# Hybrid decoder trunk: the last four experts gather their rows of X and store them over `out`; all tiles of X are loaded and stored plainly, with the loads during those experts

## The chip, the cores and the metric

The kernel runs on one core of one Trainium2 chip. The metric is the device time of one execution in microseconds (us), given as the median of several runs; two kernels are compared on the same chip.

## The reference, cut to what matters

One layer of a decoder trunk (2048 tokens, width 1024): a gated linear attention mixer, then a mixture of 64 experts in 8 groups, where each token takes two experts of one group; both are added to the residual x. A final RMSNorm gives the output.

```python
def rmsnorm(x, g):
    x32 = x.astype(jnp.float32)
    y = x32 * lax.rsqrt(jnp.mean(x32 * x32, axis=-1, keepdims=True) + EPS)
    return (y * g.astype(jnp.float32)).astype(x.dtype)
...
def hier_moe(h, w_group, w_expert, w1, w3, w2):
...
    g_sel = jnp.argmax(g_logits, axis=-1)
...
    e_prob = jax.nn.softmax(e_logits[tok, g_sel], axis=-1)
    top_p, top_i = lax.top_k(e_prob, MOE_TOPK)
...
    def expert_block(args):
        xb, e = args
        hid = jax.nn.silu(xb @ w1[e]) * (xb @ w3[e])
        return hid @ w2[e]
...
    out = jnp.zeros((n_tok + 1, dm), ys.dtype).at[slot_tok].add(ys)[:n_tok]
...
def reference(x, ...):
...
        x = x + m.astype(x.dtype)
        h = rmsnorm(x, ffn_norm[i])
        x = x + hier_moe(h, moe_w_group[i], moe_w_expert[i], moe_w1[i], moe_w3[i], moe_w2[i]).astype(x.dtype)
    return rmsnorm(x, final_norm)
```

## The kernel before

The program has four stages. The mixer (`phase_gla`) and the output projection with the router (`phase_out`) come first; the latter leaves the residual in the DRAM tensor `s["X"]` (2048 x 1024, float32), the normed rows in `s["h"]`, and in SBUF `tok` and `gate`: for each expert a column of up to 96 token numbers (a number that is no token marks an empty place) and their gates.

`phase_moe` is the third stage. Its loop runs over the experts e = 0 to 63 and one step more. Work is written out in the order in which each engine is to take it, and each engine takes its instructions strictly in that order. In step e, TensorE (PE) does the first half of expert e's up projection, turns expert e-1's hidden values (`htrans`), turns the gathered rows of expert e+1 (`xtrans`), does the second half of up, and then the down projection of expert e-1 (`down_mm`). ScalarE (ACT) and VectorE (DVE) split the weights, which arrive as tiles of 1 MB in float32, into a high and a low part (`ex.split`, L1157 and L1160), so that three matmuls replace one in float32. GpSimd (POOL) gathers the rows of expert e+4 from `s["h"]` (L1192) as soon as `xtrans(e + 1)` has freed the buffer, and adds the result of expert e-2 onto its rows of `s["X"]` (`scatter`, L1246), from the buffers `ys`. Its DMAs all go through one queue, the software queue (q0). SyncE (SP) issues the plain DMAs, in this stage the weights (L1152), through its own queue (q1). The weights live in 19 tiles of 128 x 2048 ("wide"), handed out and freed in the order of the program. When the loop is done, the last two results are scattered.

The fourth stage is `phase_more` and `phase_tail`. `phase_more` is a loop on the device over blocks of tokens that didn't fit the 96 places of an expert; with these inputs it runs no block, and its branch is skipped after all engines and all DMAs have been waited for. `phase_tail` then loads the 16 tiles of `s["X"]` (128 x 1024 each, L1396), squares and sums each on ACT (L1401), makes the inverse root for four tiles at a time (`root` on DVE and ACT, `refine` on DVE, L1406 to L1418), scales on DVE (`norm`, L1422) and stores each tile to `out` (L1423).

Of the kernel before, what the change touches and what calls it, by code (L numbers as in the profile page):

```python
# [21 lines left out]
S = 2048  # L22
# [35 lines left out]
NTAIL = 29  # L58
# [1112 lines left out]
def phase_moe(tc, c, a, s, ex, plan, rest):  # L1171
    nc = tc.nc
    with ExitStack() as ctx:
# [10 lines left out]
        scat = []  # L1184
# [55 lines left out]

        def down(e):
            Y[e] = ys[e % YS]
            nc.scalar.activation(Y[e][0:CAP, :], PD[e][0:CAP, :], AF.Copy, scale=s["gate"][0:CAP, ORDER[e]:ORDER[e] + 1])  # L1243

        def scatter(e):
            st = nc.gpsimd.indirect_dma_start(  # L1246
                out=s["X"], out_offset=bass.IndirectOffsetOnAxis(ap=tok[:, ORDER[e]:ORDER[e] + 1], axis=0),
                in_=Y[e], in_offset=None, bounds_check=S - 1, oob_is_err=False, compute_op=OP.add)
            for i, o in enumerate(scat):
# [23 lines left out]
        for e in range(E + 1):  # L1273
            live = e < E
            if e > 1:
                down(e - 2)
                scatter(e - 2)
            if live:
                up(e, 0)
# [16 lines left out]
            if e:  # L1296
                down_mm(e - 1)
            if e == 2:
                s["plan"] = plan_more(tc, s, plan)
        down(E - 1)  # L1300
        scatter(E - 1)


def plan_more(tc, s, one):
# [25 lines left out]
    total = one.tile([1, 1], I32, name="total")  # L1330
    nc.vector.tensor_copy(total, end[0:1, E - 1:E])
# [4 lines left out]
def phase_more(tc, c, a, s, slots):  # L1336

    nc = tc.nc
    with ExitStack() as ctx:
        ps = ctx.enter_context(tc.tile_pool(name="o_ps", bufs=1, space=PSUM, reuse_waits="tile"))  # L1340
        ident = c["ident"]
        tl, total, tab = s["plan"]
        w = [slots.tile(F32) for _ in range(6)]
        x, xt, y, small = own = [slots.tile(F32) for _ in range(4)]
        hid, ht = small[:, 0:FF], small[:, FF:2 * FF]
        nc.vector.memset(x, 0.0)
        n = nc.values_load(total[0:1, 0:1], min_val=0, max_val=E)
        with tc.For_i(0, n, 1) as i:
            SP = [mybir.EngineType.SP]
            e = nc.values_load(tl[0:1, bass.ds(i * 2, 1)], engines=SP, min_val=0, max_val=E - 1)  # L1350
            b = nc.values_load(tl[0:1, bass.ds(i * 2 + 1, 1)], engines=SP, min_val=0, max_val=(SLOTS - CAP) // MORE - 1)
            for k in range(6):
                nc.sync.dma_start(w[k], a["w_moe"][bass.ds(e, 1), k // 2, :, k % 2 * D:(k % 2 + 1) * D].rearrange("o p f -> p (o f)"))
            nc.sync.dma_start(tab, s["table"][CAP * E:].rearrange("(b p e) w -> b p e w", p=MORE, e=E)[
                bass.ds(b, 1), :, bass.ds(e, 1), :].rearrange("b p e w -> p (b e w)"))
            nc.gpsimd.indirect_dma_start(
                out=x, out_offset=None, in_=s["h"], in_offset=bass.IndirectOffsetOnAxis(ap=tab[:, 0:1], axis=0),
                bounds_check=S - 1, oob_is_err=False)
            for j in range(2):
                p = ps.tile([128, 512], F32, name="p", bufs=2)  # L1360
                for k in range(4):
                    nc.tensor.transpose(p[:, k * 128:(k + 1) * 128], x[:, (4 * j + k) * 128:(4 * j + k + 1) * 128], ident)
                nc.scalar.activation(xt[:, j * 512:(j + 1) * 512], p, AF.Copy)
            pu = ps.tile([128, 512], F32, name="pu")
            for k in range(NK):
                nc.tensor.matmul(pu, xt[:, k * 128:(k + 1) * 128], w[k // 2][:, k % 2 * 512:(k % 2 + 1) * 512],
                                 start=(k == 0), stop=(k == NK - 1))
            nc.scalar.activation(hid, pu[:, 0:FF], AF.Silu)
            nc.vector.tensor_tensor(hid, hid, pu[:, FF:], op=OP.mult)
            p = ps.tile([128, 256], F32, name="pt")  # L1370
            for k in range(2):
                nc.tensor.transpose(p[:, k * 128:(k + 1) * 128], hid[:, k * 128:(k + 1) * 128], ident)
            nc.scalar.activation(ht, p, AF.Copy)
            for j in range(2):
                p = ps.tile([128, 512], F32, name="p", bufs=2)
                for k in range(2):
                    nc.tensor.matmul(p, ht[:, k * 128:(k + 1) * 128], w[4 + k][:, j * 512:(j + 1) * 512],
                                     start=(k == 0), stop=(k == 1))
                nc.scalar.activation(y[:, j * 512:(j + 1) * 512], p, AF.Copy, scale=tab[:, 1:2].bitcast(F32))
            nc.gpsimd.indirect_dma_start(  # L1380
                out=s["X"], out_offset=bass.IndirectOffsetOnAxis(ap=tab[:, 0:1], axis=0),
                in_=y, in_offset=None, bounds_check=S - 1, oob_is_err=False, compute_op=OP.add)
        slots.free(*w, *own)


def phase_tail(tc, c, a, s, slots, gf):
    nc = tc.nc
    GRP = 4
    with ExitStack() as ctx:
        sm = ctx.enter_context(tc.tile_pool(name="t_sm", bufs=2, side="right", reuse_waits="tile"))  # L1390
        junk = [slots.tile(F32) for _ in range(2)]
        X, SS, R = {}, {}, {}

        def load(t):
            X[t] = slots.tile(F32)
            nc.sync.dma_start(X[t], s["X"][t * 128:(t + 1) * 128, :])  # L1396

        def square(t):
            if t % GRP == 0:
                SS[t // GRP] = sm.tile([128, GRP], F32, name="ssq")  # L1400
            nc.scalar.activation(junk[t % 2], X[t], AF.Square, accum_out=SS[t // GRP][:, t % GRP:t % GRP + 1])  # L1401

        def root(g):

            v = sm.tile([128, GRP], F32, name="v")
            nc.vector.tensor_scalar(v, SS[g], 1.0 / D, EPS, op0=OP.mult, op1=OP.add)  # L1406
            y = sm.tile([128, GRP], F32, name="r")
            nc.scalar.activation(y, v, AF.Ln)
            nc.scalar.activation(y, y, AF.Exp, scale=-0.5)
            R[g] = v, y  # L1410

        def refine(g):
            v, y = R[g]
            u = sm.tile([128, GRP], F32, name="u")
            nc.vector.tensor_tensor(u, y, y, op=OP.mult)
            nc.vector.tensor_tensor(u, u, v, op=OP.mult)
            nc.vector.tensor_scalar(u, u, -0.5, 1.5, op0=OP.mult, op1=OP.add)
            nc.vector.tensor_tensor(y, y, u, op=OP.mult)  # L1418

        def norm(t):  # L1420
            g, i = divmod(t, GRP)
            nc.vector.scalar_tensor_tensor(X[t], X[t], R[g][1][:, i:i + 1], gf, op0=OP.mult, op1=OP.mult)  # L1422
            nc.sync.dma_start(a["out"][t * 128:(t + 1) * 128, :], X[t])  # L1423

        NG = NT // GRP
        for t in range(NT):
            load(t)
        nc.scalar.preload_act_table_set(LN_EXP)
        for t in range(GRP):
            square(t)  # L1430
        root(0)
        refine(0)
        for t in range(GRP, 2 * GRP):
            square(t)
        for g in range(NG):
            if g + 1 < NG:
                root(g + 1)
                for t in range((g + 2) * GRP, min((g + 3) * GRP, NT)):
                    square(t)
            for i in range(GRP):  # L1440
                if i == GRP // 2 and g + 1 < NG:
                    refine(g + 1)
                norm(g * GRP + i)
# [3 lines left out]
def trunk(ctx, tc, a):  # L1447
# [7 lines left out]
        "todo": dram.tile([128, 2], I32, name="s_todo"),  # L1455
        "X": dram.tile([S, D], F32, name="s_X"),
# [22 lines left out]
    with ExitStack() as main:  # L1479
        big = main.enter_context(tc.tile_pool(name="tails", bufs=NTAIL, side="left", reuse_waits="tile"))  # L1480
        slots = Slots()
        slots.add(big, NTAIL)
        gf = slots.tile(F32)
        nc.sync.dma_start(gf, bass.AP(tensor=a["final_norm"].tensor, offset=a["final_norm"].offset, ap=[[0, 128], [1, D]]))
        phase_more(tc, c, a, s, slots)
        phase_tail(tc, c, a, s, slots, gf)
# [41 lines left out]
```

## Time and profile before

| | us |
|---|---|
| median of 3 runs (1597.9 to 1598.13) | 1597.99 |
| the profiled execution: its own time | 1600.11 |
| the profiled execution: its span | 1598.3 |
| PE busy in the span | 1514.1 |
| DVE / ACT / POOL busy | 1096.7 / 957.0 / 365.9 |

The span runs from the first to the last instruction of the profiled execution; the profiled execution's own time has 1.8 us more around it. Times in the views are counted from the span's start. The experts take the stretch from about 961 to 1546 us, the last stage the rest.

### The profile page before, as it was taken

What the parts mean: (1) busy time and instruction counts of PE and PEld (TensorE: products, weight loads), DVE (VectorE), ACT (ScalarE), POOL (GpSimd) and SP (SyncE); (2) the same over time, 40 slices, a digit from 0 to 9 for tenths busy, and PEclk for the clock granted to TensorE, in tenths of its full rate; (3) what the DMA queues carried; (4) which work ended last, traced back from release to release, by engine and by line L of the source; (5) the groups of instructions that cost most, each with busy time, mean ns of one, the idle gap of its engine ahead of it and who ended that gap; (6) DMA issues with size and microseconds to landing.
All of it is one profiled execution on the core that took longest, in us unless ns stands there. A gap on an engine that the chain in (4) does not pass through costs nothing.

```text
span 1598.3 us, 21450 instructions
## 1 busy us (share of the span) xinstructions
PE 1514.1 (95%) x7619; PEld 1197.2 (75%) x7619; DVE 1096.7 (69%) x2087; ACT 957.0 (60%) x1498; POOL 365.9 (23%) x265
## 2 busy tenths in 40 slices
PE   9999999999999999998999969999999999999960
PEld 7877888888888888877888856777777777777740
DVE  5566665566556655553655558889998998989955
ACT  6666644454445544441222238888888888888854
POOL 3211000000000000130111144535444444454320
PEclk9999999999999999999999979999999999999985
DMA  8645944434333433347488556999999999999969
GB/s 305 227 158 200 341 144 150 145 139 181 120 117 138 174 123 124 132 138 265 174 278 276 212 218 237 386 391 396 390 390 394 394 396 393 386 393 394 392 189 392
DMA packets 113213, 415.24 MB, mean 260 GB/s; under 512 B 23585, under 2 KB 40066, under 8 KB 88530
## 3 DMA queue, kind: packets, MB, share of 16 engines
q1 hardware_dynamic: 90242, 379.72, 61.3%
q0 software_dynamic: 19744, 33.85, 8.4%
q8 instruction: 60, 0.98, 0.2%
q10 hardware_dynamic: 3120, 0.30, 0.2%
q14 instruction: 47, 0.39, 0.1%
HBM read 353.92 MB, written 93.41 MB: 280 GB/s over the span
## 4 chain that ended last, share of the span: by engine, by line
PE 88%; DVE 5%; DMA 3%; ACT 2%; issue 1%; SPq 0%; POOL 0%; DVEq 0%; POOLq 0%; ACTq 0%
PE pm L832 9%; PE pu L77 7%; PE pu L76 7%; PE pu L75 7%; PE pvr L75 7%; PE pvr L76 7%; PE pvr L77 7%; PE pd L76 4%; PE pd L75 4%; PE pd L77 4%; PE ptr L1203 3%; PE pk L75 2%; PE pq L75 2%; PE pq L76 2%; PE pq L77 2%; PE pk L76 2%
## 5 line engine op out<-in xcount | busy, mean ns | idle before, releaser
L1160 DVE TENSOR_TENSOR wide<-wide 128x2048 fp32r<-128x2048 f32 x192 | 435.0, 2286 | 55.4 <-ACT wide L1157 46.8
L1157 ACT ACTIVATE wide<-wide 128x2048 fp32r<-128x2048 f32 x192 | 362.7, 1908 | 6.8 <-PE pd L76 6.4
L1246 POOL DMA_INDIRECT s_X<-y,tok x64 | 187.5, 2929 | 297.8 <-ACT y L1243 283.3
L75 PE MATMUL pu<-wide,xhi 128*96 128x512 f32 x512 | 207.0, 404 | 0.9 <-ACT xhi L66 0.9
L76 PE MATMUL pu<-wide,xhi 128*96 128x512 f32 x512 | 202.5, 396 | 2.2 <-DVE wide L1160 2.2
L77 PE MATMUL pu<-wide,xlo 128*96 128x512 f32 x512 | 203.6, 398 | 0.0
L75 PE MATMUL pvr<-big 128*128 128x512 f32 x504 | 201.2, 399 | 0.0
L76 PE MATMUL pvr<-big 128*128 128x512 f32 x504 | 197.1, 391 | 0.0
L77 PE MATMUL pvr<-big 128*128 128x512 f32 x504 | 196.8, 391 | 0.0
L832 PE MATMUL pm<-big 128*128 128x512 f32 x672 | 163.4, 399 | 5.4 <-DVE big L910 5.4
L67 POOL TENSOR_TENSOR big<-big 128x1024 fp32r<-128x1024 f32 x16 | 39.3, 2468 | 517.6 <-ACT big L66 458.2
L832 PEld LDWEIGHTS pm<-big 128*128 128x128 f32 x672 | 126.0, 191 | 31.4 <-DVE big L910 5.8
L77 PEld LDWEIGHTS pu<-wide,xlo 128*96 128x96 f32 x512 | 83.2, 162 | 36.7 <-DVE xlo L67 0.6
L75 PEld LDWEIGHTS pvr<-big 128*128 128x128 f32 x504 | 94.6, 188 | 20.5
L77 PEld LDWEIGHTS pvr<-big 128*128 128x128 f32 x504 | 94.6, 188 | 20.3
L76 PEld LDWEIGHTS pu<-wide,xhi 128*96 128x96 f32 x512 | 83.7, 164 | 34.5 <-DVE wide L1160 2.9
L66 ACT ACTIVATE sp<-st 128x256 fp32r<-128x256 f32 x64 | 26.7, 417 | 136.5 <-DVE st L455 124.4
L76 PEld LDWEIGHTS pvr<-big 128*128 128x128 f32 x504 | 94.7, 188 | 18.0
L75 PEld LDWEIGHTS pu<-wide,xhi 128*96 128x96 f32 x512 | 83.3, 163 | 32.6 <-ACT xhi L66 1.2
L75 PE MATMUL pd<-wide,ht 128*96 128x512 f32 x256 | 100.8, 394 | 1.3 <-ACT ht L66 1.3
L77 PE MATMUL pd<-wide,ht 128*96 128x512 f32 x256 | 100.7, 393 | 0.0
L76 PE MATMUL pd<-wide,ht 128*96 128x512 f32 x256 | 100.6, 393 | 0.0
(298 smaller groups left out, 2860.6 us busy)
## 6 DMA issues: line engine op xcount, KB each, us to landing
wide<-w_moe SPq DMA_DIRECT2D x192, 1024.0 KB
big<-s_hT SPq DMA_DIRECT2D x96, 512.0 KB
s_hT<-big SPq DMA_DIRECT2D x32, 512.0 KB
s_oT<-big SPq DMA_DIRECT2D x32, 512.0 KB
big<-s_oT SPq DMA_DIRECT2D x32, 512.0 KB
big<-x SPq DMA_DIRECT2D x20, 512.0 KB
big<-w_vr SPq DMA_DIRECT2D x16, 512.0 KB
s_X<-big SPq DMA_DIRECT2D x16, 512.0 KB
```

The costliest lines, as they stand in the source:

```text
L66: nc.scalar.activation(hi, src, AF.Copy)
L67: eng.tensor_tensor(lo, src, hi.bitcast(F32), op=OP.subtract)
L75: nc.tensor.matmul(out, x[0], w[0], start=start, stop=False)
L76: nc.tensor.matmul(out, x[0], w[1], start=False, stop=False)
L77: nc.tensor.matmul(out, x[1], w[0], start=False, stop=stop)
L832: self.nc.tensor.matmul(pm[i], xo[:, sl], w[:, i * 512:(i + 1) * 512], start=(k == 0 and w is whi and xo is hi), stop=(k == NK - 1 and xo ...
L1157: self.nc.scalar.activation(hi, r, AF.Copy)
L1160: self.nc.vector.tensor_tensor(lo, r, hi.bitcast(F32), op=OP.subtract)
L1203: nc.tensor.transpose(p[:, k, 0:CAP], x[0:CAP, k * 128:(k + 1) * 128], ident[0:CAP, 0:CAP])
L1246: st = nc.gpsimd.indirect_dma_start(out=s["X"], out_offset=bass.IndirectOffsetOnAxis(ap=tok[:, ORDER[e]:ORDER[e] + 1], axis=0), in_=Y[e], ...
```

## The change

The fourth stage is gone as a stage of its own, and its work is written into the end of `phase_moe`.

- The experts 60 to 63 (`LAST = 4`) no longer scatter onto `s["X"]`. Their rows of `s["X"]` are gathered (`xgather`, in steps 60 and 61) into the buffers `ys` and `xbs[1]`; DVE adds gate times result onto them (`final`, in place of `down` on ACT), ACT squares them (`final_square`), and after the closing norm (`final_norm`, DVE) GpSimd stores the rows to `out` by their numbers (`put_out`), after the 16 plain stores, whose stale rows they replace.
- The 16 tiles of `s["X"]` are loaded in eight loads of 1 MB into freed weight tiles (`load_final`, from step 61 on). They wait for the last scatter, that of expert 59.
- The squares of the tiles 0 and 1 stand in step 63 on ACT, those of 2 to 15 behind the loop, mixed with `root`, `refine` and `norm`.
- `targets` (step 3) and `targets_in` (step 6) are new. The first writes the numbers of all tokens to a DRAM tensor `s["dst"]` and overwrites those of the last four experts' tokens; the second brings them back into SBUF, turns them on PE and copies them to `dst`. With `MASK = False`, nothing reads `dst`.
- The loop over blocks that didn't fit now stands at the very end, inside a branch that is taken only if there are such blocks, and then does the closing norm over.

```diff
+LAST = 4
+GRP = 4
+MASK = False
...
+        def targets():
+
+            nc.gpsimd.iota(rows, pattern=[[1, 128]], base=0, channel_multiplier=128, allow_small_or_imprecise_dtypes=True)
+            nc.gpsimd.memset(none, NSENT)
+            nc.gpsimd.dma_start(s["dst"].rearrange("(t p) w -> t (p w)", p=128), rows)
...
+            for e in range(E - LAST, E):
+                st = nc.gpsimd.indirect_dma_start(
+                    out=s["dst"], out_offset=bass.IndirectOffsetOnAxis(ap=tok[:, ORDER[e]:ORDER[e] + 1], axis=0),
+                    in_=none, in_offset=None, bounds_check=S - 1, oob_is_err=False)
...
+        def targets_in():
+            nc.gpsimd.dma_start(rows, s["dst"].rearrange("(t p) w -> t (p w)", p=128))
+            p = ps.tile([128, 2, 128], F32, name="pht")
+            nc.tensor.transpose(p[:, 0, 0:NT], rows, ident[0:NT, 0:NT])
+            nc.vector.tensor_copy(dst, p[:, 0, 0:NT])
...
+        def final(e):
+            f = fin[e][0:CAP, :]
+            nc.vector.scalar_tensor_tensor(f, PD[e][0:CAP, :], s["gate"][0:CAP, ORDER[e]:ORDER[e] + 1], f, op0=OP.mult, op1=OP.add)
...
+                XP[j] = ex.tile(F32)[0].rearrange("p (i d) -> p i d", i=2)
+                nc.sync.dma_start(XP[j], s["X"][256 * j:256 * (j + 1), :].rearrange("(i p) d -> p i d", p=128))
...
-            if e > 1:
+            if 1 < e < E - LAST + 2:
                 down(e - 2)
                 scatter(e - 2)
+            elif e > 1:
+                final(e - 2)
+            if e == E - LAST:
+                xgather(E - 4)
+            elif e == E - LAST + 1:
+                for i in range(1, LAST):
+                    xgather(E - LAST + i)
...
+            if e == E - 1:
+                nc.scalar.preload_act_table_set(LN_EXP)
...
             if e:
                 down_mm(e - 1)
+            if e > E - LAST + 1:
+                final_square(e - 2)
+            if e > E - LAST:
+                load_final()
+            if e == E - 1:
+                square(0)
+                square(1)
             if e == 2:
                 s["plan"] = plan_more(tc, s, plan)
-        down(E - 1)
-        scatter(E - 1)
+            elif e == 3:
+                targets()
+            elif e == 6:
+                targets_in()
+        square(2)
+        square(3)
+        root(0)
+        refine(0)
+        norm(0)
+        final(E - 1)
+        norm(1)
...
+        fs = []
+        for g in range(1, NT // GRP):
+            refine(g)
+            for i in range(GRP):
+                t = (g + 1) * GRP + i
+                if t < NT:
+                    square(t)
+                if i == GRP - 1 and g + 1 < NT // GRP:
+                    root(g + 1)
+                norm(g * GRP + i)
+                if len(fs) < LAST and i % 2:
+                    fs.append(final_norm(E - LAST + len(fs)))
+        if not MASK:
+            for i, f in enumerate(fs):
+                put_out(f, tok[:, ORDER[E - LAST + i]:ORDER[E - LAST + i] + 1])
```

How the instructions stand. On POOL, in the steps 3 to 6 of the changed kernel (`s_X<-y` is a scatter, `xb<-s_h` a gather of an expert's rows; line numbers are those of the changed kernel):

```order
L1359 DMA s_X<-y_9321,tok 2048x1024
L1198 DMA xb_9318<-s_h,tok 128x1024
L1255 IOTA rows 16x128
L1256 MEMSET none 128x1
L1257 DMA s_dst<-rows 16x128
L1260 DMA s_dst<-none,tok 2048x1 x4
L1359 DMA s_X<-y_9322,tok 2048x1024
L1198 DMA xb_9319<-s_h,tok 128x1024
L1359 DMA s_X<-y_9320,tok 2048x1024
L1198 DMA xb_9317<-s_h,tok 128x1024
L1359 DMA s_X<-y_9321,tok 2048x1024
L1198 DMA xb_9318<-s_h,tok 128x1024
L1268 DMA rows<-s_dst 16x128
```

Between step 3's gather and step 4's scatter stand seven new instructions, five of them DMAs, and one more DMA stands behind step 6's gather; the scatters and gathers themselves keep their order.

On PE, at the end of step 6 of the changed kernel (`pd` is expert 5's down projection, `pu` expert 7's up projection):

```order
L77 MATMUL pd<-wide,ht 96x512
L78 MATMUL pd<-wide,ht 96x512
L79 MATMUL pd<-wide,ht 96x512
L1270 MATMUL pht<-ident,rows 128x16
L77 MATMUL pu<-wide,xhi 96x512
L78 MATMUL pu<-wide,xhi 96x512
```

One small transpose, of what L1268 brings in, stands between the two experts' matmuls; before, `pu` followed `pd` directly.

On ACT, from step 63's activation (`sg`) to the last `ht`, in the kernel before:

```order
L1220 ACTIVATE sg<-pu 96x256
L1157 ACTIVATE wide<-wide 128x2048
L1243 ACTIVATE y_9321<-pd,gate 96x1024
L66 ACTIVATE ht<-pht 128x2x96
L1243 ACTIVATE y_9319<-pd,gate 96x1024
```

Here `ht`, for which PE's last down projection waits, has one split and one scaling (`y<-pd`) ahead of it. The same place in the changed kernel, up to the first root:

```order
L1226 ACTIVATE sg<-pu 96x256
L1411 ACT_TABLE_LOAD
L1159 ACTIVATE wide<-wide 128x2048
L1290 ACTIVATE xb_9317,stats<-y_9321 96x1024
L1308 ACTIVATE xb_9317,stats<-wide 128x1024 x2
L68 ACTIVATE ht<-pht 128x2x96
L1290 ACTIVATE xb_9317,stats<-y_9322 96x1024
L1308 ACTIVATE xb_9317,stats<-wide 128x1024 x2
L1315 ACTIVATE r<-v 128x4
L1316 ACTIVATE r<-r 128x4
```

The two scalings are gone; a table load and three squares (`stats<-`) now stand ahead of the last `ht`, and the first root follows three squares behind it.

## Rows read from the trace of the kernel before

**Rows 1.** The page, part 1: busy us, share of the span, instructions.
```profile
PE 1514.1 (95%) x7619; PEld 1197.2 (75%) x7619; DVE 1096.7 (69%) x2087; ACT 957.0 (60%) x1498; POOL 365.9 (23%) x265
```

**Rows 2.** Waits of PE from 1000 to 1545 us: total us, times, longest.
```profile
PE pd L75 <- ACT ht L66: 1.3, 1, 1.3
```

**Rows 3.** Busy us by stretch, then granted TensorE clock, DMA share, GB/s.
```profile
1500.00:1520.00 20.00, 20.00 (x102) 14.46 (x101) 18.13 (x15) 17.56 (x16) 8.23 (x4) 1.00 1.02 399
...
1557.60:1568.50 10.90, 0.00 (x0) 0.00 (x0) 0.96 (x7) 9.31 (x18) 0.00 (x0) 0.50 1.01 407
1568.50:1598.30 29.80, 0.00 (x0) 0.00 (x0) 21.02 (x31) 9.70 (x22) 0.00 (x0) 0.50 0.95 386
```

**Rows 4.** The chain that ended last, near its end: start us, us, what.
```profile
1547.68 5.71 DMA s_X<-y,tok
...
1557.64 9.46 DMA big<-s_X
```

**Rows 5.** PE in time, end of step 6: start us, us, what.
```profile
1020.43 0.39 PE L77 MATMUL pd<-wide,ht 128*96 128x512 f32 x1
```

**Rows 6.** POOL in time: first gather; step 6's scatter and gather; [idle before <-releaser].
```profile
940.60 1.06 POOL L1192 DMA_INDIRECT xb<-s_h,tok  x1 [19.84 <-DVE seen L998]
...
1014.70 3.60 POOL L1246 DMA_INDIRECT s_X<-y,tok  x1 [5.21 <-ACT y L1243]
1018.60 2.57 POOL L1192 DMA_INDIRECT xb<-s_h,tok  x1 [0.30 <-issue]
```

**Rows 7.** PE in time: the transposes of the first gather's rows.
```profile
950.12 1.51 PE L1203 MATMUL ptr<-ident,xb 96*128 96x96 f32 x8 [4.64 <-DMA xb<-s_h,tok]
```

**Rows 8.** DMA queue q0 from 1018, 1021 and 1025 us: packets, MB, share.
```profile
q0 software_dynamic: 33, 0.00, 0.6%
...
q0 software_dynamic: 122, 0.26, 33.1%
...
q0 software_dynamic: 161, 0.24, 16.3%
```

**Rows 9.** PE in time: 24 matmuls before and 24 after a wait.
```profile
715.31 5.73 PE L832 MATMUL pvr<-big 128*128 128x512 f32 x24
726.46 8.57 PE L832 MATMUL pm<-big 128*128 128x512 f32 x24 [5.42 <-DVE big L910]
```

**Rows 10.** All engines in time, from step 63's activation to the end.
```profile
1538.88 0.38 ACT L1220 ACTIVATE sg<-pu 96x256 f32<-96x256 f32 x1 [2.45 <-PE pu L77]
...
1539.16 1.90 ACT L1157 ACTIVATE wide<-wide 128x2048 fp32r<-128x2048 f32 x1
...
1542.66 0.32 ACT L66 ACTIVATE ht<-pht 128x192 fp32r<-128x192 f32 x1
...
1547.68 1.55 POOL L1246 DMA_INDIRECT s_X<-y,tok  x1 [2.88 <-ACTq L1348]
1554.05 13.39 SPq L1396 DMA_DIRECT2D big<-s_X  x16
1554.14 1.28 ACT L1428 ACT_TABLE_LOAD   x1 [6.74 <-DMA s_X<-y,tok]
1557.82 1.06 ACT L1401 ACTIVATE big<-big 128x1024 f32<-128x1024 f32 x1 [2.39 <-DMA big<-s_X]
...
1559.07 1.06 ACT L1401 ACTIVATE big<-big 128x1024 f32<-128x1024 f32 x1
...
1563.25 0.17 DVE L1406 TENSOR_SCALAR v<-ssq 128x4 f32<-128x4 f32 x1 [18.53 <-ACT big L1401]
...
1564.53 0.16 DVE L1418 TENSOR_TENSOR r<-r,u 128x4 f32<-128x4 f32 x1
...
1569.77 20.58 SPq L1423 DMA_DIRECT2D out<-big  x16
...
1573.99 2.47 DVE L1422 SCALAR_TENSOR_TENSOR big<-big,r 128x1024 f32<-128x1024 f32 x2
```

**Rows 11.** Waits of SP at the end: total us, times, longest.
```profile
SPq L1524 <- DMA out<-big: 6.7, 1, 6.7
```

More of the change, by code (lines that the diff above doesn't have):

```diff
@@ L1183, in phase_moe @@
         spacer = wk.tile([1, 2], F32, name="spacer2", bufs=1)
-        scat = []
+        scat, outs, xg = [], [], []
+        rows = xp.tile([NT, 128], F32, name="rows")
+        none = xp.tile([128, 1], F32, name="none")
         XT, HID, UP, HT, PD, Y = {}, {}, {}, {}, {}, {}
@@ new lines, in refine, with put_out @@
+        def refine(g):
+            v, y = R[g]
+            u = wk.tile([128, GRP], F32, name="u")
+            nc.vector.tensor_tensor(u, y, y, op=OP.mult)
+            nc.vector.tensor_tensor(u, u, v, op=OP.mult)
+            nc.vector.tensor_scalar(u, u, -0.5, 1.5, op0=OP.mult, op1=OP.add)
+            nc.vector.tensor_tensor(y, y, u, op=OP.mult)
+        def put_out(x, index):
+            st = nc.gpsimd.indirect_dma_start(
+                out=a["out"], out_offset=bass.IndirectOffsetOnAxis(ap=index, axis=0),
+                in_=x, in_offset=None, bounds_check=S - 1, oob_is_err=False)
+            for o in outs:
+                tc.declare_no_dep(st.ins, o.ins, reason="a row of out is written by its last expert or with its tile")
+            outs.append(st)
@@ new lines, in phase_moe @@
+        root(0)
[3 more added lines that the diff above has]
+        norm(1)
+        square(4)
+        final_square(E - 1)
+        root(4)
+        square(5)
+        refine(4)
+        norm(2)
+        square(6)
+        norm(3)
+        square(7)
+        root(1)
+        fs = []
[10 more added lines that the diff above has]
+                    fs.append(final_norm(E - LAST + len(fs)))
@@ new lines, in phase_moe @@
+        if not MASK:
+            for i, f in enumerate(fs):
+                put_out(f, tok[:, ORDER[E - LAST + i]:ORDER[E - LAST + i] + 1])
+        tl, total, tab = s["plan"]
+        ws = [ex.tile(F32)[0] for _ in range(3)]
+        x = ex.tile(F32)[0]
+        x, xt = x[:, 0:D], x[:, D:]
+        y = ex.tile(F32)[0]
+        y, hid, ht = y[:, 0:D], y[:, D:D + FF], y[:, D + FF:D + 2 * FF]
+        some = nc.values_load(total[0:1, 1:2], min_val=0, max_val=1)
+        n = nc.values_load(total[0:1, 0:1], min_val=0, max_val=E)
@@ new lines, in phase_moe @@
+        with tc.For_i(0, some, 1):
+            for e in range(E - LAST, E):
+                nc.gpsimd.indirect_dma_start(
+                    out=s["X"], out_offset=bass.IndirectOffsetOnAxis(ap=tok[:, ORDER[e]:ORDER[e] + 1], axis=0),
+                    in_=fin[e], in_offset=None, bounds_check=S - 1, oob_is_err=False)
+            nc.vector.memset(x, 0.0)
+            with tc.For_i(0, n, 1) as i:
+                block(tc, a, s, i, ps, c["ident"], tl, tab, ws, x, xt, y, hid, ht)
+            for t in range(NT):
+                xs = XP[t // 2][:, t % 2, :]
+                nc.sync.dma_start(xs, s["X"][t * 128:(t + 1) * 128, :])
+                square(t)
+            nc.scalar.preload_act_table_set(LN_EXP)
+            for g in range(NT // GRP):
+                root(g)
+                refine(g)
+                for i in range(GRP):
+                    xs = XP[2 * g + i // 2][:, i % 2, :]
+                    nc.vector.scalar_tensor_tensor(xs, xs, R[g][1][:, i:i + 1], s["gf"], op0=OP.mult, op1=OP.mult)
+                    t = g * GRP + i
+                    nc.sync.dma_start(a["out"][t * 128:(t + 1) * 128, :], xs)
@@ L1338, in phase_more @@
     nc = tc.nc
[L1339 to L1383, printed above, removed]
@@ L1386, in phase_tail @@
[L1386 to L1443, printed above, removed]
@@ new lines, in block @@
+    nc.gpsimd.indirect_dma_start(
+        out=x, out_offset=None, in_=s["h"], in_offset=bass.IndirectOffsetOnAxis(ap=tab[:, 0:1], axis=0),
+        bounds_check=S - 1, oob_is_err=False)
+    p = ps.tile([128, NK, 128], F32, name="ptr")
+    for k in range(NK):
+        nc.tensor.transpose(p[:, k, :], x[:, k * 128:(k + 1) * 128], ident)
+    nc.scalar.activation(xt, p.rearrange("p k i -> p (k i)"), AF.Copy)
+    pu = ps.tile([128, 512], F32, name="pu", bufs=2)
+    for k in range(NK):
+        nc.tensor.matmul(pu, xt[:, k * 128:(k + 1) * 128], w[k // 2][:, k % 2 * 512:(k % 2 + 1) * 512],
+                         start=(k == 0), stop=(k == NK - 1))
@@ new lines, in block @@
+    nc.scalar.activation(hid, pu[:, 0:FF], AF.Silu)
+    nc.vector.tensor_tensor(hid, hid, pu[:, FF:], op=OP.mult)
+    p = ps.tile([128, 2, 128], F32, name="pht")
+    for k in range(2):
+        nc.tensor.transpose(p[:, k, :], hid[:, k * 128:(k + 1) * 128], ident)
+    nc.scalar.activation(ht, p.rearrange("p k i -> p (k i)"), AF.Copy)
+    p = ps.tile([128, D], F32, name="pd")
+    for j in range(2):
+        for k in range(2):
+            nc.tensor.matmul(p[:, j * 512:(j + 1) * 512], ht[:, k * 128:(k + 1) * 128], w[4 + k][:, j * 512:(j + 1) * 512],
+                             start=(k == 0), stop=(k == 1))
```

88 lines of the change are left out of this document (75 added, 13 removed).

## The prediction

> **What bounds the kernel now.** I read the page's busy times first: PE is busy 95% of the span [rows 1]. A mean over stages doesn't say where, so the waits come next. Between 1000 and 1545 us, nearly all of the expert stage, PE waits once, for 1.3 us, in front of the last down projection [rows 2]. [...] So the experts run at PE's pace; a pause of PE there can't be made up and moves the end by its whole length. The last stage has another limit. PE has nothing to do, and the DMA engines are full (shares 1.01 and 0.95, 407 and 386 GB/s) [rows 3]: 8.4 MB of X come in, 8.4 MB go out. Ahead of it, in the chain that ended last, the final scatter takes 5.71 us until it has landed, at 1553.39, and the first loads follow [rows 4]. What the change can win is there, between 1546 and 1598 us; what it can lose is any new wait of PE.
>
> **The marks written in step 3 (`targets`).** Five DMAs more on POOL, some 1.06 us each [rows 6], and the second waits until the first has landed. For that landing I take 9.5 us, the time from the first gather's issue at 940.60 [rows 6] to the transposes that waited for it at 950.12 [rows 7]. Together 5 x 1.06 + 9.5 = 15 us, behind which step 4's scatter and gather queue. That gather serves PE in step 7, three steps of 9.1 us later (64 experts in 585 us), and 15 + 9.5 is under 27. The lead of the gathers covers it: 0. Without that cover PE would wait for what is over.
>
> **The numbers brought back in step 6 (`targets_in`).** This is the term that decides. PE's transpose stands directly behind expert 5's down projection, whose last matmul ends at 1020.43 + 0.39 = 1020.8 [rows 5]. What it waits for is issued on POOL behind step 6's gather, which ends at 1018.60 + 2.57 = 1021.2 [rows 6]; with the 0.30 us that stand ahead of such an issue, 1021.5. So the copy isn't even issued when PE asks for it. When does it land? It goes through the software queue behind the scatter of 1014.70 and the gather of 1018.60 [rows 6]. That queue moves nothing from 1018 to 1021 us, 0.26 MB from 1021 to 1025 and 0.24 MB from 1025 to 1029 [rows 8]: one scatter's and one gather's worth of rows, each some 6 us after its issue. The copy can hardly move before 1029. I take the 9.5 us of the first gather, also under a full DMA: 1021.5 + 9.5 = 1031.0, and PE pauses 1031.0 - 1020.8 = 10.2 us. From below, the copy takes as long as a plain load into an empty queue, 3.8 us (X load issued at 1554.05, its square at 1557.82 [rows 10]): pause 4.5. From above, the marks have put the queue one scatter (4 us) further behind: pause 14. I stay at 10.2, since the first gather ran under the same full DMA and the empty queue is not this stage's. Behind the transpose on PE is all of the rest; DVE's copy of the result stands behind splits that are done by then, and waits along.
>
> [...]
>
> **The clock after it.** A wait of 5.42 us stands ahead of 24 matmuls that take 8.57 us; the 24 of the same shape before it take 5.73 [rows 9]. So a pause of this kind costs 2.8 us more while PE runs at the lower level. I take 2.8 once; 0 from below, twice that from above.
>
> **The steps 61 to 63.** Step 62 gives DVE one more instruction of about 1.24 us (half of 2.47 for two scalings of 128 x 1024 [rows 10]; the trace shows none that adds from PSUM). With 18.13 of 20 us taken [rows 3] that is up to 0.4 us a step more than there is, for two steps. I count 0, at most 1. The gathers of X replace scatters one for one.
>
> **The end.** I follow the engines from ACT's `sg` of step 63, which ends at 1538.88 + 0.38 = 1539.3. Then come, in this order, a table load (1.28), a split (1.90), six squares at 1.25 (from one square's start to the next's) and `ht` (0.32) [rows 10]: 11.0, so 1550.3. A root with its refine takes 1564.69 - 1563.25 = 1.4: 1551.7. PE's last down projection waits for `ht` 3.5 us longer than now, until 1546.5; its 12 matmuls (half of 5.73, or of 8.57 at worst) are done before DVE asks, behind the first scaling, at 1553.0. Loads: they go behind the last weights, which have landed when their split begins at 1539.16 now [rows 10]. With 3.8 us to the first landing the first tile is there at 1543.0; its square comes at 1543.7, and 8.4 MB at 407 GB/s bring a tile each 1.29 us. So the loads are hidden, and a late one would cost its lateness.
>
> From 1551.7 on DVE sets the pace: 16 scalings and 4 of the experts' rows at 1.24 make 24.7, the addition for expert 63 1.2, four more refines at 0.65 (four instructions of 0.16 to 0.17) 2.6, and one more wait for a root 1.5: 30.0, so 1581.7. The last store lands 3.8 us later, as a load into a queue that is no longer full: 1585.5. Only then may the four `put_out` start. Such plain row stores aren't in the trace. From below they cost what a gather does, 1.06 with 0.30 between; from above what a scatter under load does, 3.60 [rows 6]. I take the gather, because the DMA is empty then, and the last scatter of now, with the DMA nearly empty, took 1.55 [rows 10]: 5.4, so 1590.9. From the end of that last scatter to its landing are 5.71 - 1.55 = 4.2 [rows 4, 10]: 1595.1. The branch over the loop takes 1554.05 - 1553.39 = 0.7, and from the last landing to the end of the span are 1598.3 - (1590.35 + 6.7) = 1.25 [rows 10, 11]: 1597.0. The end wins 1.3 us. That is little because DVE's 25 us of scalings were hidden under the DMA's work and now stand open, and because the stores by row can't overlap with the plain ones.
>
> **Sum,** against the profiled span: 1598.3 + 10.2 + 2.8 - 1.3 = 1610.0, 11.7 more. The median lies 0.3 under that span, so 1597.99 + 11.7 = 1609.7 us.
>
> **Rivals.** *The copy comes quickly.* Then PE pauses 4.5 us: 1604.0. For it speaks that it has 16 rows only; against it that its queue holds two transfers of 0.25 MB [rows 8]. [...] The chance is 12%.
> *PE's pause is made up* (the other side). If the DMA, with its share of 1.02 [rows 3], is what the experts really keep pace with, the weights run ahead during the pause and PE gets the time back: the end alone counts, 1597.99 - 1.3 = 1596.7, no change. It decides as soon as PE has waits for weights to give up; against it, PE has none in 545 us [rows 2]. 7%.
> *The end is worth more.* If the stores and not DVE set its pace, 8.4 MB at 386 GB/s take 21.7 us from 1551.7 and the end wins 30.0 - 21.7 = 8.3 more: 1601.4. Against it stand the 24.7 us of scalings. 6%.
> *The row stores are slow,* 3.90 us each as under load: 10.2 more, 1619.9. For it speaks that they wait for full queues to drain; against it the 1.55. 10%.
>
> **How the numbers follow.** The forecast has 65%, with its own range from 1603 (pause 4.5, no clock cost) to 1616 (pause 14 and the forecast's clock, rounded up for the step 62). For 8 in 10 the range takes in the quick copy and the better end, down to 1600, and half of the slow row stores, up to 1618; left out are the made-up pause and most of the slow stores. A measurement of this kernel tells 0.2%, 3.2 us, from no change. Slower than that: forecast, quick copy, slow stores, less a little of the quick copy with a better end, 84%. Within it: the made-up pause and half of the better end, 10%. Faster: better end with a quick copy, 6%.
>
> **What would show it.** Right: PE's transpose in step 6 waits some 10 us for a DMA onto `rows`, the granted clock falls to 0.5 for a few us behind it, and all later experts are some 13 us late; behind the last matmul DVE is busy without gaps for some 30 us, and the last 11 us hold four stores by row. Wrong: no wait of PE near 1021 us, or one under 5 us; squares that wait for loads; row stores of 3 us or more; a last scaling before 1578 or behind 1586 us, counted from the unshifted start.

## The result, and the profile after

The changed kernel takes 1615.28 us (median of 4 runs, 1612.16 to 1620.98), the kernel before 1598.06 beside it: 1.0108 times as long, 95% interval 1.0079 to 1.0138. The profiled execution took 1620.98 us with a span of 1619.0; it is the slowest of the four, the others have spans of 1610.2 to 1613.9.

The page of the changed kernel, part 1, answers to [rows 1]:

```profile
PE 1519.0 (94%) x7620; PEld 1198.9 (74%) x7620; DVE 1106.8 (68%) x2102; ACT 958.6 (59%) x1504; POOL 381.7 (24%) x277
```

The span is 20.7 us longer, but PE is busy only 4.9 us more. So PE stood idle. Where, the waits of PE from 960 to 1600 us show (what waited <- for what: total us, times, longest):

```profile
PE pht L1270 <- DMA rows<-s_dst: 16.8, 1, 16.8
PE pd L77 <- ACT ht L68: 4.2, 1, 4.2
PE pu L78 <- DVE wide L1162: 2.1, 2, 1.9
```

[Rows 2], which begin at 1000 us, had one wait of 1.3 us, for the last `ht`; it is 4.2 us now. The 2.1 us lie before 1000 us, and the kernel before has 2.2 there. New is one transpose that waits 16.8 us. PE in time, around it:

```profile
1021.12 0.40 PE L79 MATMUL pd<-wide,ht 128*96 128x512 f32 x1
1038.29 0.25 PE L1270 MATMUL pht<-ident,rows 16*128 16x16 f32 x1 [16.78 <-DMA rows<-s_dst]
1038.47 0.74 PE L77 MATMUL pu<-wide,xhi 128*96 128x512 f32 x1
1039.01 0.63 PE L78 MATMUL pu<-wide,xhi 128*96 128x512 f32 x1
1039.44 0.63 PE L79 MATMUL pu<-wide,xlo 128*96 128x512 f32 x1
```

PE asks at 1021.52 and gets the numbers at 1038.29. Behind the pause the matmuls stand 0.43 us apart, before it 0.23: the lower clock. The table by stretch (columns as in [rows 3]) has its level of 0.50 until about 1043 and 1.00 again from 1046 us on; and while PE stands still, the DMA engines fill every free weight tile and then have nothing to do (shares 0.92, 0.02, 0.35; SP waits 21.8 us for a matmul on `pu` before it issues the next load):

```profile
1034.00:1038.00 4.00, 0.00 (x0) 0.00 (x0) 0.00 (x0) 0.00 (x0) 0.00 (x0) 0.50 0.92 290
1038.00:1042.00 4.00, 3.71 (x10) 2.51 (x10) 0.17 (x1) 0.00 (x0) 0.00 (x0) 0.50 0.02 3
1042.00:1046.00 4.00, 4.00 (x22) 3.01 (x21) 0.89 (x2) 1.71 (x3) 1.05 (x1) 0.82 0.35 82
1046.00:1050.00 4.00, 4.00 (x19) 2.77 (x18) 3.15 (x4) 3.83 (x4) 0.00 (x0) 1.00 0.83 313
```

Why so late? POOL in time, from the marks of step 3 to the copy (L1257 is the store of all numbers, L1260 the marks, L1359 a scatter, L1198 a gather, L1268 the copy back):

```profile
991.80 0.57 POOL L1257 DMA_DIRECT2D s_dst<-rows  x1 [0.24 <-POOL none L1256]
999.26 1.07 POOL L1260 DMA_INDIRECT s_dst<-none,tok  x1 [6.88 <-DMA s_dst<-rows]
1000.63 2.86 POOL L1260 DMA_INDIRECT s_dst<-none,tok  x1 [0.30 <-issue]
1003.79 4.41 POOL L1260 DMA_INDIRECT s_dst<-none,tok  x1 [0.30 <-issue]
1008.51 0.98 POOL L1260 DMA_INDIRECT s_dst<-none,tok  x1 [0.31 <-issue]
1009.80 3.45 POOL L1359 DMA_INDIRECT s_X<-y,tok  x1 [0.30 <-ACT wide L1159]
...
1015.56 3.44 POOL L1359 DMA_INDIRECT s_X<-y,tok  x1 [0.31 <-issue]
...
1022.18 4.96 POOL L1359 DMA_INDIRECT s_X<-y,tok  x1 [0.31 <-issue]
1027.44 1.05 POOL L1198 DMA_INDIRECT xb<-s_h,tok  x1 [0.30 <-issue]
1028.49 0.58 POOL L1268 DMA_DIRECT2D rows<-s_dst  x1
```

The scatters of the steps 4 and 5 in the kernel before, POOL in time as well (step 6's is in [rows 6]):

```profile
995.36 4.16 POOL L1246 DMA_INDIRECT s_X<-y,tok  x1 [4.71 <-ACT y L1243]
...
1005.57 2.58 POOL L1246 DMA_INDIRECT s_X<-y,tok  x1 [2.68 <-ACT y L1243]
```

The idle times in brackets show why. Before, POOL waits 2.7 to 5.2 us in each step for ACT's result; after the marks it waits for nothing (0.30), because it is behind. Step 4's scatter starts 14.4 us later than before (1009.80 - 995.36), step 5's 10.0, step 6's 7.5. When PE asks, POOL is still 7.0 us from issuing the copy. It lands 9.8 us after its issue: 7.0 + 9.8 = 16.8.

The end, all engines in time, answers to [rows 10]:

```profile
1559.61 0.38 ACT L1226 ACTIVATE sg<-pu 96x256 f32<-96x256 f32 x1 [2.43 <-PE pu L79]
...
1571.83 1.28 DVE L1338 SCALAR_TENSOR_TENSOR wide<-wide,r 128x1024 f32<-128x1024 f32 x1
...
1597.19 4.87 DVE L1338 SCALAR_TENSOR_TENSOR wide<-wide,r 128x1024 f32<-128x1024 f32 x4
1606.61 1.01 POOL L1328 DMA_INDIRECT out<-wide,tok  x1 [56.85 <-SPq L1475]
...
1610.53 0.98 POOL L1328 DMA_INDIRECT out<-wide,tok  x1 [0.30 <-issue]
```

Step 63's `sg` ends at 1559.99, 20.73 later than the 1539.26 of before, and the span ends 20.7 later: the new end is worth nothing, neither gain nor loss.

### The profile page after: what moved, and what is told of

The parts are those of the page before. It is cut to its first block, busy times and chain, and to the rows that moved or that the text cites. A ratio compares the mean times of both kernels' runs of the same rounds, so it can differ in the third digit from the quotient of the medians.

```text
span 1619.0 us, 21503 instructions
## 1 busy us (share of the span) xinstructions
PE 1519.0 (94%) x7620; PEld 1198.9 (74%) x7620; DVE 1106.8 (68%) x2102; ACT 958.6 (59%) x1504; POOL 381.7 (24%) x277
## 5 line engine op out<-in xcount | busy, mean ns | idle before, releaser
L1359 POOL DMA_INDIRECT s_X<-y,tok x60 | 179.2, 2986 | 264.8 <-ACT y L1356 256.3
L69 POOL TENSOR_TENSOR big<-big 128x1024 fp32r<-128x1024 f32 x16 | 39.3, 2466 | 519.0 <-ACT big L68 457.8
```

Source lines behind the costliest of these rows:

```text
L69: eng.tensor_tensor(lo, src, hi.bitcast(F32), op=OP.subtract)
L1359: st = nc.gpsimd.indirect_dma_start(out=s["X"], out_offset=bass.IndirectOffsetOnAxis(ap=tok[:, ORDER[e]:ORDER[e] + 1], axis=0), in_=Y[e], ...
```

## The experiments

The theory: the whole loss is PE's pause in step 6. Its length is POOL's lateness with the copy (the marks' doing) plus 9 to 10 us until it has landed; the clock comes on top. The rivals: the marks or the last steps cost something themselves, or the pause has another cause. Medians of the kernel before stand beside each run, from the same chip; the parts of a pause are read from one profiled execution of each kernel.

**Without the numbers.** Steps 3 and 6 lose their new work; the end stays.

```diff
             if e == 2:
                 s["plan"] = plan_more(tc, s, plan)
-            elif e == 3:
-                targets()
-            elif e == 6:
-                targets_in()
```

> Without the marks of step 3 and the numbers brought back in step 6; all else as in the changed kernel. Theory A, the pause of PE in step 6 with its clock is the whole loss and the new end is worth about nothing: PE doesn't wait in front of expert 7, and the time is that of the kernel before within 2 us, 1596 to 1600. Theory B, the end itself is slower and the pause only adds to it: 1603 or more. Theory C, the pause had been made up in part later: over 1600.

Measured: 1599.28 (11 runs) against 1598.95; ratio 1.0000, 0.9991 to 1.0009. The numbers, which nothing reads, are all of the loss. From PE's end of step 6 to the end of step 63's `sg` this kernel takes 519.0 us, the one before 518.4. These 0.6 us grow little by little over all the steps, for a reason that stays open; from step 58's `sg` to step 63's both take 45.1 us, so the steps 61 to 63 cost nothing.

**The marks alone.**

```diff
-            elif e == 6:
-                targets_in()
```

> The marks of step 3 stay, the numbers aren't brought back in step 6. Theory A, late gathers and scatters after the marks are hidden by their lead of three steps: POOL is some 7 us late in step 6 as in the changed kernel, PE doesn't wait, 1596 to 1600. Rival, the marks cost time of their own because a gather comes too late: a wait of PE for a gather in step 7 or 8 and 1601 to 1606.

Measured: 1600.36 (10 runs); ratio 1.0002, 0.9993 to 1.0011, and PE has no wait near step 7. POOL is late all the same: its gather of step 6 ends at 1026.44 us, before at 1021.17. The marks alone are hidden, as the prediction had it; the median is 0.4 over the range, but not told from no change.

**The copy back alone.** The four indirect marks go; the store of all numbers and the copy stay.

```diff
-            for e in range(E - LAST, E):
-                st = nc.gpsimd.indirect_dma_start(
...
-                ws.append(st)
```

> The numbers are written in step 3 and brought back in step 6, without the four marks between (nothing reads the result). Theory A, the marks put POOL 7 us back and that made the pause 16.8 us and not 10: the copy is issued near 1021.5, PE pauses 9 to 11 us, and the time is 1608 to 1612, some 5 us under the changed kernel. Rival, the length of the pause comes from the full DMA alone and not from POOL's lateness: a pause of 15 us or more and 1613 to 1617.

Measured: 1613.66 (4 runs, 1611.66 to 1614.29); ratio 1.0089, 1.0074 to 1.0105. PE's wait and, in the second fence, POOL in time:

```profile
PE pht L1263 <- DMA rows<-s_dst: 9.4, 1, 9.4
```

```profile
1017.06 2.59 POOL L1198 DMA_INDIRECT xb<-s_h,tok  x1 [0.30 <-issue]
1019.65 0.57 POOL L1261 DMA_DIRECT2D rows<-s_dst  x1
```

Without marks POOL is on time: the copy is issued 0.35 us after PE asks, lands 9.04 later, and the pause is 9.4. That is the picture that the prediction had of the changed kernel itself. The time doesn't follow as well: the median is above the 1608 to 1612 of theory A and in the range of its rival. The profiled execution (1611.66) is the quickest of the four; why the others take up to 2.6 us more stays open. (In the profiled executions step 3's `sg` ends between 988.6 and 991.1 us, so differences of this size arise before any new work.) Against the kernel before, this kernel loses 14.7 us, the changed one 17.2 and, run again, 18.5: by the medians the marks' lateness costs 2.5 to 3.8 us, by the profiled pauses 5.0 to 7.4.

**The transpose four steps later.** The copy stays in step 6; PE and DVE take it in step 10.

```diff
+        def turn():
             p = ps.tile([128, 2, 128], F32, name="pht")
...
             elif e == 6:
                 targets_in()
+            elif e == 10:
+                turn()
```

> Marks and numbers as in the changed kernel, the copy issued in step 6 too, but PE's transpose and DVE's copy stand in step 10. Theory A, only the place of the transpose costs, the work itself nothing: no wait of PE, 1596 to 1600, the same as without the numbers. Rival, the work on POOL and in the software queue costs in itself: 2 us or more over the kernel without the numbers.

Measured: 1601.10 (10 runs); ratio 1.0011, 1.0001 to 1.0020. The pause is gone, with all the numbers still made and brought in; the median lies between the two expectations, 1.8 us over the first experiment. PE's waits show what is left:

```profile
PE pht L1233 <- DVE dst L1273: 1.2, 1, 1.2
```

The next transposes of PE need the PSUM tile (`pht`, which PE's transposes write) that DVE reads for `dst`, and DVE's copy stands behind its splits in the program.

**The changed kernel again,** unaltered.

> The changed kernel once more, unaltered, to see how much the pause varies between executions. Theory A (the pause is how late POOL is with the issue of the copy, plus some 9 to 10 us until it has landed): issue between 1021.5 and 1028.5 us, pause between 10 and 17 us, median 1612 to 1617. Rival (16.8 us was an accident of the one profiled execution, the usual pause is the 10.2 us of the prediction): pause about 10, median 1608 to 1611.

Measured: 1616.01 (4 runs, 1614.78 to 1617.75) against 1597.49; ratio 1.0112, 1.0096 to 1.0127. The pause is 14.4 us this time, with POOL 5.1 us late:

```profile
1022.28 3.89 POOL L1198 DMA_INDIRECT xb<-s_h,tok  x1 [0.30 <-issue]
1026.18 0.57 POOL L1268 DMA_DIRECT2D rows<-s_dst  x1
```

**The copy and transpose in step 9,** the marks in step 3.

```diff
-            elif e == 6:
+            elif e == 9:
                 targets_in()
```

> The marks stay in step 3; the copy back, with the transpose, is issued in step 9 instead of step 6, when POOL no longer has a backlog. Theory A (the marks cost only through the backlog that they leave on POOL): the copy is issued within 1 us of PE's last matmul, lands some 9 us later, PE pauses 9 to 10 us, the median is that of the kernel without the marks, 1611 to 1614. Rival (the marks themselves hold the copy, by their own landing or their bytes in the queue): pause 14 to 17 us as in the changed kernel, median 1614 to 1618. Second rival (with the queue calm the copy lands as fast as an empty one): pause 4 us, median 1603 to 1605.

Measured: 1609.95 (4 runs, 1608.94 to 1611.13) against 1597.49; ratio 1.0079, 1.0064 to 1.0094. POOL has no backlog any more (its scatter waits 4.68 us for ACT again) and issues the copy before PE asks at 1046.53:

```profile
1039.87 3.11 POOL L1359 DMA_INDIRECT s_X<-y,tok  x1 [4.68 <-ACT y L1356]
1043.28 1.05 POOL L1198 DMA_INDIRECT xb<-s_h,tok  x1 [0.30 <-issue]
1044.34 0.57 POOL L1268 DMA_DIRECT2D rows<-s_dst  x1
```

The pause is 8.1 us and the median a little below the range that theory A gave, because the copy is issued 2.2 us before PE asks. The rival by which the marks themselves hold the copy falls: they are all there. So does the one of the calm queue (4 us). The executions together (us; "asked" is the end of PE's last matmul ahead of the transpose, "landed" the transpose's start):

| kernel | asked | issued | landed | late | landing | pause |
|---|---|---|---|---|---|---|
| prediction | 1020.8 | 1021.5 | 1031.0 | 0.7 | 9.5 | 10.2 |
| changed | 1021.52 | 1028.49 | 1038.29 | 7.0 | 9.8 | 16.8 |
| changed, again | 1021.09 | 1026.18 | 1035.53 | 5.1 | 9.35 | 14.4 |
| no marks | 1019.30 | 1019.65 | 1028.69 | 0.35 | 9.0 | 9.4 |
| copy in step 9 | 1046.53 | 1044.34 | 1054.64 | -2.2 | 10.3 | 8.1 |

The landing is much the same in each; what differs is when POOL comes to issue it. In the changed kernel the copy lands just as the DMA engines run out of work, but that isn't its cause: without the marks it lands at 1028.69, and their share is 1.03 from 1026 to 1030 us and 1.01 from there to 1034. In each of the four executions 16 packets of 512 bytes move between issue and landing, as many as the copy has; in that of the changed kernel none of them moves before 1035.4 us, 6.9 us after the issue. Whether they stand behind the transfers ahead of them in the queue, or the full DMA engines delay them otherwise, isn't shown.

**The copy issued by SP** instead of POOL, at the same place in the program.

```diff
-            nc.gpsimd.dma_start(rows, s["dst"].rearrange("(t p) w -> t (p w)", p=128))
+            nc.sync.dma_start(rows, s["dst"].rearrange("(t p) w -> t (p w)", p=128))
```

> The changed kernel, with the copy back issued by SP through its queue instead of by POOL through the software queue; place in the program, marks and transpose are unchanged. Theory A (the pause is POOL's lateness of 5 to 7 us, plus the 9 to 10 us that a small transfer needs behind the indirect ones in the software queue): the copy no longer stands behind POOL's scatters and gathers, and it lands after the marks and at most two weight tiles of 1 MB (some 2.6 us each at 400 GB/s); PE pauses 0 to 8 us, median 1599 to 1609. Rival (any transfer takes 9 to 10 us in this stretch, since the DMA is full): PE pauses 9 to 10 us, or more if SP, waiting for the marks, holds the weights back as well; median 1611 to 1617.

Measured: 1617.62 (4 runs) against 1598.78; ratio 1.0122, 1.0101 to 1.0142. Both expectations of the pause failed; it is 16.6 us. SP has no wait for the marks, which the rival named as a reason for more. SP's queue in time, and the DMA queues from 1019.36 to 1034 us (packets, MB, share):

```profile
994.85 24.34 SPq L1154 DMA_DIRECT2D wide<-w_moe  x12
1019.36 0.33 SPq L1268 DMA_DIRECT2D rows<-s_dst  x1
1040.92 18.88 SPq L1154 DMA_DIRECT2D wide<-w_moe  x7
```

```profile
q1 hardware_dynamic: 592, 4.09, 67.4%
q0 software_dynamic: 654, 1.18, 33.4%
```

The issue is on time, 0.3 us after PE asks at 1019.08, but it lands 16.3 us later, at 1035.69. I had counted two weight tiles ahead of it. SP issues nothing more until 1040.92, so the 4.1 MB that its queue (q1) moves in this time were issued ahead of the copy: nearly four tiles. POOL's rows (q0) take another 1.2 MB of the DMA engines' work. The DMA engines' share is 0.96 to 1.04 in each 4 us from 1018 to 1034 and 0.03 from there to 1038; the copy lands in that last stretch. The lateness was cured and the landing got worse; the median is as bad as that of the changed kernel.

**The end without the row stores** (and without the numbers). The rows of the last four experts' tokens stay stale.

```diff
-        if not MASK:
-            for i, f in enumerate(fs):
-                put_out(f, tok[:, ORDER[E - LAST + i]:ORDER[E - LAST + i] + 1])
```

> As the changed kernel without marks and numbers, and without the four stores by row at the end; the rows of the last four experts' tokens are left stale in the output. Theory A, these stores stand open behind the last plain store, four times 1.3 us, the landing of the last and the waits around them: 9 to 11 us less than the kernel without the numbers, 1586 to 1590. Rival, the end is set by the plain stores still draining, and the stores by row hide behind them: 0 to 3 us less.

Measured: 1590.88 (4 runs) against 1598.78; ratio 0.9951, 0.9933 to 0.9969. Against the first experiment this is 8.4 us less by the medians, and 8.6 from the end of step 63's `sg` to the end of the span (50.3 against 58.9): the four row stores stand open with all but a little of what was expected (9 to 11).

**All tiles stored by row** (`MASK = True`, with the late transpose), so that the row stores needn't wait for plain ones.

```diff
-MASK = False
+MASK = True
```

> The numbers are used: all tiles go out by row on POOL, each without the rows of the last four experts' tokens, so that the stores of those rows need not wait for the others; the numbers are turned in step 10. Theory A, the last 11 us were the wait between the two kinds of stores: the end is DVE's last scaling plus one store, 1588 to 1592. Rival, a store by row takes POOL 2.5 to 3.5 us under load, 20 of them then set the pace of the end: 1605 or more, with DVE waiting for nothing and POOL busy to the end.

Measured: 1600.14 (10 runs); ratio 1.0008, 0.9998 to 1.0018. POOL in time, first and last of 20:

```profile
1555.66 1.82 POOL L1330 DMA_INDIRECT out<-wide,dst  x1 [23.62 <-DVE wide L1340]
...
1583.32 2.02 POOL L1330 DMA_INDIRECT out<-wide,tok  x1 [0.30 <-DVE wide L1340]
...
1589.48 0.98 POOL L1330 DMA_INDIRECT out<-wide,dst  x1 [0.30 <-issue]
```

DVE's last scaling ends at 1584.49; POOL is then four stores behind, and from its last to the end of the span are 9.7 us, where the first experiment has 7.4. What the overlap wins (46.1 instead of 47.0 us from the first scaling to the end) the late transpose has cost already. Both expectations failed: the end is not one store behind the last scaling, and the 20 stores don't take 2.5 to 3.5 us each.

**The gain on POOL, the last scaling of the experts' rows on ACT** (without the numbers), to relieve DVE.

```diff
-            nc.vector.scalar_tensor_tensor(f, fin[e], R[4][1][:, i:i + 1], s["gf"], op0=OP.mult, op1=OP.mult)
+            nc.gpsimd.tensor_tensor(fin["out", i // 2][:, i % 2, :], fin[e], s["gf"], op=OP.mult)
...
+            nc.scalar.activation(f, f, AF.Copy, scale=R[4][1][:, i:i + 1])
```

> As the changed kernel without marks and numbers, with the gain of the four experts' rows multiplied on POOL and their scale on ACT, so that DVE has four scalings less at the end. Theory A, DVE's 20 scalings set the pace of the end: 4 to 5 us less than without the numbers, 1592 to 1595. Rival, the stores set the pace or POOL's multiplications slow DVE down: within 2 us of the kernel without the numbers.

Measured: 1600.97 (10 runs); ratio 1.0012, 1.0003 to 1.0022. No gain, within 2 us of the first experiment, as the rival had it. DVE's waits in the end show part of why: ACT's squares, into which its four scalings are now put (in the first experiment the same line has 3.4):

```profile
DVE v L1313 <- ACT xb L1308: 6.4, 4, 3.1
```

DVE has four scalings less, and its last one still ends 31.9 us behind the start of its first, instead of 30.2. Another 2.0 us go to one small instruction that stands under POOL's multiplication, as the last fence of this document shows. The experiment moves work to two engines at once, so it doesn't tell what either move alone would do.

**Three last experts instead of four** (without the numbers).

```diff
-LAST = 4
+LAST = 3
...
-        fin = dict(zip(range(E - LAST, E), ys + xbs[1:]))
+        fin = {E - 3: ys[(E - 3) % YS], E - 2: ys[(E - 2) % YS], E - 1: xbs[1]}
...
-                xgather(E - 4)
+                xgather(E - LAST)
```

> Without the numbers, and with three experts instead of four that keep their rows back: one scaling, one square and one row store less at the open end, the loads of X wait for one scatter more. Theory A (the end is DVE's scalings and then POOL's row stores, one behind the other; the loads have time to spare): 1.2 + 1.3 = 2.5 us less than the kernel without the numbers, median 1596 to 1598. Rival (the loads set the pace as soon as they wait for one scatter more): no gain or a loss, median 1599 to 1604, with ACT's squares waiting for the loads.

Measured: 1596.80 (11 runs) against 1597.49; ratio 0.9995, 0.9986 to 1.0004. DVE's last scalings and POOL's stores come 1.2 and 2.5 us sooner than in the first experiment, as expected:

```profile
1574.63 4.87 DVE L1338 SCALAR_TENSOR_TENSOR wide<-wide,r 128x1024 f32<-128x1024 f32 x4
```

It has the lowest time of the complete variants against the kernel before and takes 1.2% less than the changed kernel. It is shown neither to be faster than the kernel before nor than the first experiment: of the 2.5 us that the profile has, the medians show about 1, within their intervals.

## Why the prediction was right, and where it was off

It forecast 1609.7 us, in a range of 1600 to 1618; 1615.28 is slower than before, as forecast, and 5.6 above the number. That it lies in the range is in part luck. The terms of the range don't add up to its bounds: a pause of 4.5 without the clock makes 1601.2 and not 1603, a pause of 14 with 1 us for step 62 makes 1614.5 and not 1616. The room above, up to 1618, was there for slow row stores, which didn't come; both profiled pauses of the changed kernel are longer than the 14 us at most.

- **The bound** was right. PE's pause moved everything behind it by its whole length: of the 20.73 us at step 63, 0.70 were there already at step 6 (PE's last `pd` of it ends at 1021.52 instead of 1020.82), 17.1 are the pause with its transpose (expert 7's first `pu` starts at 1038.47, and 0.23 behind the `pd` ahead of it would have been 1021.35), 2.9 are left. The rival by which weights that run ahead make it up is refuted by the run itself: they did run ahead until the DMA engines had nothing to do, and PE got nothing back.
- **The marks** are hidden, as forecast. But their price was taken too low: 15 us were forecast, and from the gather's end at 991.28 to the last mark's end at 1009.49 are 18.2. The store landed sooner than assumed (7.5 us from issue to the first mark); the marks took 1.0 to 4.4 us each instead of 1.06.
- **The pause** is the step that failed: 10.2 us forecast, at most 14, and 16.8 and 14.4 measured. The forecast took the time of the copy's issue from POOL's rows of before ([rows 6], 1021.5), although the paragraph above it put 15 us of new work in front of them; the marks' lateness stood in the upper bound alone, as one scatter of 4 us, and it was 7.0 and 5.1. That the lead of the gathers hides this work says that PE doesn't wait for a gather. It doesn't say that POOL is on time again three steps later. Of the 9.1 us of a step POOL had 2.7 to 5.2 to spare before, so 14.4 us of lateness shrink to 7. The experiment without marks comes close to the forecast's issue, landing and pause (0.35, 9.0, 9.4), so nothing else in this step was wrong. The profiled executions are the slowest of their four runs both times; with the clock, the end and the rest as measured below, a loss of 17.2 us would mean a pause of some 14 (an estimate: 17.2 less 2.3, 0.6 and 0.3 for the transpose).
- **The landing** of 9.5 us held: 9.0 to 10.3 in four executions. None of them comes near the 3.8 us of a plain load, from which the quick copy was worked out, and that rival falls.
- **The clock,** 2.8 forecast, 2.3 measured (behind the wait of [rows 9] the granted clock is 0.50 from 725.8 to 732.6 us and 1.00 from there to 739): step 7's `sg` ends 20.16 us later than before (1047.77 against 1027.61), and 0.70 and 17.1 of it are named above. Worked out alike, the three other executions with a pause in the table have 2.0, 3.0 and 1.5. The other 0.6 of the 2.9 come by and by until step 63, as in the experiment without the numbers, where PE doesn't pause; the prediction has no term for them.
- **The end,** −1.3 forecast, 0 measured. Counted from step 63's `sg`, the first scaling was forecast at 12.4 and came at 11.8; the last one's end at 42.4 and 42.1; the first row store at 46.2 and 46.6; the end of the last at 51.6 and 51.5. Only the last piece was clearly mis-sized: from there to the end of the span 7.5 us, not 6.1. The row stores took 1.0 us each, as chosen from the two bounds.

## What to carry to other kernels

Work that is hidden by a lead still makes its engine late, and whatever else that engine issues starts from the late time: carry the backlog forward, step by step, with the idle time that each step leaves, to the next place where somebody waits without a lead. An engine that takes its instructions in order, as PE did here with expert 7's matmuls behind one transpose for 16.8 us, should meet a transfer's result some steps behind its issue: four steps between copy and transpose turned a loss of 1.1% into one of 0.1%. And moving a small transfer to another queue need not bring it sooner: here it landed 16.3 us after its issue, with 4.1 MB of prefetched weights issued ahead of it in that queue, instead of 9.0 to 10.3.

## What the runs showed of the hardware

POOL's indirect DMAs take 1.0 us (a scatter 1.6) or up to 5, and the trace shows what goes with it: a split of DVE that is already running. DVE in time, in the changed kernel, beside the rows of POOL above:

```profile
991.69 2.27 DVE L1162 TENSOR_TENSOR wide<-wide 128x2048 fp32r<-128x2048 f32 x1
...
1000.32 2.29 DVE L1162 TENSOR_TENSOR wide<-wide 128x2048 fp32r<-128x2048 f32 x1 [0.50 <-ACT wide L1159]
...
1002.86 4.49 DVE L1162 TENSOR_TENSOR wide<-wide 128x2048 fp32r<-128x2048 f32 x2
...
1009.50 2.29 DVE L1162 TENSOR_TENSOR wide<-wide 128x2048 fp32r<-128x2048 f32 x1 [0.85 <-ACT wide L1159]
...
1015.24 2.29 DVE L1162 TENSOR_TENSOR wide<-wide 128x2048 fp32r<-128x2048 f32 x1 [0.91 <-ACT y L1356]
...
1021.19 4.48 DVE L1162 TENSOR_TENSOR wide<-wide 128x2048 fp32r<-128x2048 f32 x2
```

The splits from 1000.32 on end at 1002.61, 1007.35, 1011.79, 1017.53 and 1025.67. The marks that were running end 0.88 and 0.85 us later (1003.49, 1008.20), the scatters 1.46, 1.47 and 1.47 later (1013.25, 1019.00, 1027.14). So in these five POOL's instruction ends 0.85 to 0.88 us (a mark) or 1.46 to 1.47 us (a scatter) after DVE's split, whether it has taken 2.86 us or 4.96. The order of starts tells which are held up: from 960 us on, 73 of the changed kernel's indirect DMAs start while a split or a scaling runs, and 72 of them are longer than their kind takes alone (scatters 2.60 to 4.96 us, the others 1.52 to 4.42); the other 60 start beside none and none of them is longer (scatters 1.59 to 1.65 us, the others 0.98 to 1.07), though 51 see a split or a scaling start. The one plain DMA of POOL that starts under a split isn't held: the store of 991.80 starts under the split of 991.69 and takes 0.57 us, the copy of 1028.49, with DVE idle, 0.58. In the end, with DVE idle, each row store takes 0.98 to 1.01 us; of the 20 beside scalings and behind them (`MASK = True`), eight took 1.59 to 2.02 us and twelve 0.97 to 1.00. Had I read [rows 6] for it, the marks would have been priced by the splits beside them. No run here took the splits away from under the marks, so the cause is argued from these starts and ends and not shown by an edit.

The other way round was seen once, in the experiment with the gain on POOL (all engines in time):

```profile
1554.18 3.31 POOL L1348 TENSOR_TENSOR wide<-xb,wide 128x1024 f32<-128x1024 f32 x1 [5.13 <-DVE xb L1286]
...
1555.36 2.15 DVE L1313 TENSOR_SCALAR v<-stats 128x4 f32<-128x4 f32 x1
```

An instruction of DVE on 128 x 4 numbers that takes 0.17 us elsewhere takes 2.15 and ends at 1557.51, with POOL's multiplication (1557.49).
